# Batch-normalised matmul on one core: two output blocks turned by DMA, one more chunk of x copied apart, and a re-timed, re-ranked instruction plan

## The chip, the core and the metric

The kernel runs on one core of one Trainium2 chip. Its engines work side by side, each through its own list of instructions in order: TensorE (PE, matmuls and transpositions by matmul), VectorE (DVE), ScalarE (ACT), GpSimd (POOL) and SyncE (SP). Here SP's list holds nearly nothing but DMA issues (all stores and all transpositions by DMA); POOL's list holds the loads of x and of the weight beside its arithmetic. Sixteen DMA engines carry the transfers. The metric is the device time of one execution in microseconds, smaller being better; the median of three runs of the kernel before is 205.97 us (205.72 to 206.15).

## The reference

```
x: (16, 512, 1024) f32      weight: (1024, 768) f32      gamma, beta: (768,)
y      = matmul(x, weight)                       # 8192 rows x 768 columns
mean   = y.mean over all 8192 rows; var = y.var over all 8192 rows   (per column)
out    = gamma * (y - mean) / sqrt(var + eps) + beta
```

No output column can be written before all 8192 rows of that column are computed, since the mean and the variance run over all of them. x has 33.5 MB, the output 25.2 MB.

## The kernel before, in words

**Tiling.** The 8192 rows are cut into 16 chunks of 512 (C, CH), the 768 columns into 6 tiles of 128 (NT). All matmuls run in bf16. Columns 0 to 255 (tiles 0 and 1, "GA") are computed with rows on the partitions (`mm_rows`, L510, 256 columns wide); their sums are kept on DVE and POOL, and for the last two chunks they are computed with columns on the partitions (`ga_unit`, L814). Tiles 2 to 5 are computed with columns on the partitions: 8 matmuls of 512 rows for each chunk and tile (`mm`, L575), statistics by DVE (L711) or, for tile 2, partly by ACT (L720, L724), and a copy of y to SBUF in bf16.

**Loads and turning of x.** POOL's DMAs load x chunk by chunk and cast it to bf16 (`load_x`, L403). DVE turns it in 32x32 blocks so that k lies on the partitions (`turn_x`). For most chunks the turn moves pairs of bf16 as one 32-bit word, so in the result the two values of a pair lie next to each other and a matmul reads x with a step of two elements. Chunks in SINGLE (2, 3, 6) are turned value by value and read with step one. Chunks in PARTED (4, 5, 7 to 10) are copied apart after the turn: `part_chunk` has four ACT copies (L547) from `xT_sb` to `x_pl`, and all later matmuls of that chunk read `x_pl`. Chunks 12 to 15 (LATE) are copied apart later, by ACT or DVE. Chunks 0, 1 and 11 are read in pairs for all tiles.

**From y to the output.** Tiles 2 to 5 hold columns on the partitions and have to be turned back by 128x128 blocks. The unit is a block of two chunks (1024 rows, 512 KB of output). Three ways are used (`col_block`, `raw_turn`):
- "pe": normalise on DVE, 8 transpositions on TensorE into PSUM (`turn_block`, L1044; they may be threaded one by one between matmuls of other work, "hosted"), ACT copies PSUM to the f32 ring (L1210), SP stores.
- "xact": normalise (ACT for tile 2, DVE for tiles 3 and 4), one DMA transposition on SP's queue (L1220) from SBUF to SBUF, ACT converts bf16 to f32 (L1232), SP stores (L1202).
- RAW: the raw y is turned by a DMA transposition first (L1106), and normalised afterwards with rows on the partitions by DVE (L1174) and POOL (L1178), stored at L1182.

Before the change tile 2 has chunks 0-1 and 2-3 raw and its other blocks "xact", tile 3 has chunks 0-1 raw and the others "xact", and tile 4 has chunks 0-1, 2-3 and 4-5 raw and its other blocks "pe", the last one held back for the end ("held", L1252). Tile 5 is the tail: after the last matmul (L753) its statistics are closed, and all 16 chunks are normalised (L1348), turned on TensorE (L1044), copied by ACT (L1361) and stored (L1364). Columns 0 to 255 need no turning: DVE multiplies (L937), POOL or DVE adds (L942), SP stores (L946).

**What sets the order.** The kernel first collects some 790 tasks. Each has a priority, the engines it may run on with a time (busy, then until its result can be used), the tasks it waits for, and the buffers that it takes and uses. `arrange` plays these tasks through on a model of the five engines and of the DMA (`Wires`): again and again it takes the engine that can begin first, and of the tasks that can begin on it within 0.2 us the one with the smallest priority. The resulting list is the order in which instructions are written, engine by engine, and the chip keeps that order. So a changed duration or priority changes no work, only which instruction stands before which on each engine and each queue. Priorities are mostly due times: `clock`, which adds up TensorE's planned time, plus an offset. Turns of x have -1000 added, so that they always rank first.

**Buffers.** Turned chunks of x, parted copies and the tail's output share 12 buffers (XT); PSUM has 8 banks; the ring in SBUF holds loads of x and blocks of output.

Of the kernel before, what the change touches and what calls it, by code (L numbers as in the profile page):

```python
# [9 lines left out]
class Task:  # L10
# [3 lines left out]
    def __init__(self, prio, engines, emit, deps=(), dma=None, uses=(), takes=()):  # L14
# [6 lines left out]
        self.slack = self.look = 0.0  # L21
        for slot in self.uses + self.takes:
            slot.users.append(self)
# [74 lines left out]
class Wires:  # L98
# [4 lines left out]
    def __init__(self):  # L103
        self.free = 4.3
        self.lanes = {"SP": [], "POOL": [], "ACT": []}
# [5 lines left out]
    def send(self, queue, t, hold, took, count):  # L111

        soft = queue == "POOL"
        for _ in range(count):
            t = max(t, self.ready(queue)) + hold / count
            self.free = max(self.free, t + (1.0 if soft else 0.5)) + took / count
            land = self.free + (1.3 if soft else 0.6)
            self.lanes[queue].append(land)
        return t, land


def arrange(tasks, turns, log=None):
# [8 lines left out]
    SEM, LOOK = 0.06, 0.2  # L131
# [36 lines left out]
    while left:  # L168
# [46 lines left out]
        if t.dma:  # L215
            free[e], t.end = wires.send(e, start, occ, t.dma, t.count)
# [11 lines left out]
def kernel(  # L228
# [46 lines left out]
    PARTED, LATE, SINGLE = (4,5,7,8,9,10), (12,13,14,15), (2,3,6)  # L275
    MODE = {2:'xact',3:'xact',4:('pe',)*8}
# [98 lines left out]
    STORE, XBAR = 1 / 350.0, 1.25  # L375
# [72 lines left out]
    for kind, n, *n1 in order:  # L448
# [12 lines left out]
        if m0 == M // 2:  # L461
# [5 lines left out]
            t, {"POOL": (2.68 * rows / CH + 0.535 * also, 2.68 * rows / CH + 0.535 * also)}, load_x(m0, rows, slot, between),  # L467
# [5 lines left out]
        for i in range(rows // QR):  # L473
            c, q = divmod(m0 // QR + i, QPC)
            for j0, j1 in ((0, JW // 2), (JW // 2, JW)) if m0 < CH else ((0, JW),):
                new = q == 0 and j0 == 0
                x_ready[c, q, j1] = task(
                    -1000 + t, dve((2.2 if c in SINGLE else 1.16) * (j1 - j0) / JW + 0.02),
# [5 lines left out]
        if rows % QR:  # L484
# [4 lines left out]
                -1000 + t, dve(0.63), turn_x(slot, x_slot[c], m0, t0, 0, JW, False, P),  # L489
# [159 lines left out]
    def rows_stats(c, ts, slot, t):  # L649
# [30 lines left out]
        s = task((now + 4.2 if c < RC - 2 else 0), {"POOL": (1.36, 1.36 + 0.05), "DVE": (0.62, 0.7)}, add_squares, [a],  # L680
# [124 lines left out]
    def ga_unit(nt, c, q, cols=QR):  # L805
# [26 lines left out]
        b = task(clock[0] - late, dve(0.609 * cols / CH + 0.05), bn, [t], uses=[slot])  # L832
        mine = [h[1] for k, h in ga_half.items() if k[1] == c]
        k = task(clock[0] + 3.4, act(0.48 * cols / CH + 0.03), keep, [b] + mine,
# [20 lines left out]
    merges.append(task(U, dve(0.36), merge(0), [k[1] for k in ends], True))  # L855
    merges.append(task(U, pool(0.65), merge(1), [k[2] for k in ends]))
    for h in range(2):
        merges.append(task(U, pool(0.65), more(h), merges[1:]))
# [59 lines left out]
    s1 = task(U, pe(0.9), sums_rows, merges, takes=[tot_slot])  # L918
    se = task(U, dve(0.8), sums_entry, [s1], True, uses=[tot_slot])
    ag = [task(U, dve(0.25), aggregate_rows(a), [se] + [h[0] for k, h in ga_half.items() if k[0] == a]) for a in range(GA)]  # L920
    rt = task(U, {"ACT": (0.2, 0.3)}, root_rows, ag)
    sc = task(U, dve(0.3), scale_rows, [rt], True)
    sr = task(U + 0.1, dve(0.35), shift_rows, [sc], True)
    p0 = task(U, pe(0.45), spread_rows(0), [sc], takes=[a0_slot])
    p1 = task(U, pe(0.45), spread_rows(1), [sr], takes=[a1_slot])
    p1.look = 0.6
    sh = task(U, act(0.3), shift_sbuf, [p1], uses=[a1_slot])


    def rows_out(c, s0, s1, k):  # L930
# [19 lines left out]
        a = task(due, dve(0.3 * n), norm, [p0] + keeps, takes=[slot], uses=[y_row[c], a0_slot])  # L950
        b = task(due + 0.4, dve(0.3 * n) if k in ADDED else pool(0.59 * n), add, [a, p1 if k in ADDED else sh],
                 uses=[slot, a1_slot] if k in ADDED else [slot])
        task(due + 1.0, {"SP": (0.38, 0.4)}, store, [b], dma=n * NA * P * 4 / 1024 / 365.0 * 1.024,
# [14 lines left out]
    def finish_tasks(nt):  # L968
# [41 lines left out]
        if nt in ASTAT:  # L1010
            deps = [task(now + 1.0, {"ACT": (1.2, 1.3)}, total, deps)]
        a = task(now + 1.0, dve(0.5), var, deps)
        b = task(now + 1.0, {"ACT": (0.2, 0.3)}, root, [a])
        if nt > GA:
            return task(now + 1.0, dve(0.55), affine, [b], True)
# [396 lines left out]
```

## Time and profile before

| quantity | value |
|---|---|
| timed runs | 205.97 us median, 205.72 to 206.15 |
| span of the profiled execution (its first to its last instruction) | 204.1 us |
| the median less that span | 1.9 us |
| PE busy | 189.3 us (93%), 1210 matmuls and transpositions |
| DVE, ACT, POOL busy | 159.3, 146.2, 124.1 us |
| chain that ended last | PE 86%, ACT 3%, DMA 3%, POOL 2% |
| HBM read, written | 36.71 MB, 25.17 MB |
| mean granted TensorE clock | 0.979 |
| ACT copies apart, L547 | 32, mean 1063 ns (8 more on DVE, mean 715 ns) |
| ACT conversions after a DMA transposition, L1232 | 13, mean 1063 ns |
| ACT copies after TensorE's turning, L1210 | 4, mean 1014 ns |
| TensorE transpositions of tiles 4 and 5, L1044 | 104 |
| DMA transpositions L1220, issue to landing | 13, median 4.4 us |
| stores of 512 KB from the ring, issue to landing | 37, median 3.4 us |

How to read it: times are in microseconds from the start of the span. An engine's busy time counts its own instructions alone. The chain is followed back from the last instruction to what released it, each time, so what stands in it is what the end hangs on. The DMA share is the mean share of 16 engines, and because packets overlap it can pass 1; where transfers are of one kind the GB/s tell better whether the engines are full. Before 100 us the loads run, from 110 us on the stores.

### The profile page before, as it was taken

The numbers are of one execution on the slowest core, as the hardware profiler recorded it, in microseconds if no ns is written. First come the engines' busy times: TensorE is split into PE (matmuls) and PEld (weight loads), VectorE is DVE, ScalarE is ACT, GpSimd is POOL, SyncE is SP. The second block draws the span as 40 slices with busy tenths as digits, with TensorE's granted clock in tenths as the row PEclk, the third lists the DMA queues.
The fourth block names the chain that finished last, engine by engine and source line by source line (L and its number), as shares of the span: only waits on it lengthen the run. The fifth ranks groups of instructions, "written<-read, shape, count | busy, mean of one in ns | idle before, by whom it ended". The sixth has DMA issues, their size and how long they took to land.

```text
span 204.1 us, 3510 instructions
## 1 busy us (share of the span) xinstructions
PE 189.3 (93%) x1210; PEld 114.5 (56%) x1210; DVE 159.3 (78%) x250; ACT 146.2 (72%) x260; POOL 124.1 (61%) x150
## 2 busy tenths in 40 slices
PE   7969999999999999999999999999999999997900
PEld 3457554657488888777865444444444445544600
DVE  4031879999999999969989998987999878657900
ACT  2001461368989999899978766999998959956950
POOL 7776954877499989997403999389613312940000
PEclk9999999999999999999999999999999999999965
DMA  4999999999999999999686899899999999999998
GB/s 71 172 199 196 176 196 196 196 197 197 190 193 197 197 196 196 196 197 195 103 181 200 297 339 336 248 301 328 295 322 227 336 303 274 347 343 310 310 347 253
DMA packets 98562, 48.74 MB, mean 239 GB/s; under 512 B 24304, under 2 KB 98032, under 8 KB 98544
## 3 DMA queue, kind: packets, MB, share of 16 engines
q0 software_dynamic: 34624, 18.36, 65.5%
q1 hardware_dynamic: 63920, 30.16, 52.6%
q8 instruction: 9, 0.15, 0.3%
q14 instruction: 9, 0.07, 0.1%
HBM read 36.71 MB, written 25.17 MB: 303 GB/s over the span
## 4 chain that ended last, share of the span: by engine, by line
PE 86%; ACT 3%; DMA 3%; POOL 2%; issue 1%; ACTq 0%; DVE 0%; POOLq 0%
PE y_ps L575 54%; PE y_ps L510 24%; PE y_ps L814 4%; ACT o_sb L1361 3%; DMA ring<-in_x_dram 3%; PE o_ps L1044 1%; POOL ring L403 1%; POOL w_sb L387 1%; PE y_ps L753 1%; PE a_ps L903 1%; PE o_ps L1074 0%; ACTq L1407 0%; PE idle_ps L591 0%; PE tot_ps L871 0%; ACT ring L1252 0%
## 5 line engine op out<-in xcount | busy, mean ns | idle before, releaser
L575 PEld LDWEIGHTS <-w_sb 128*128 128x128 bf16 x520 | 50.3, 97 | 57.6
L575 PE MATMUL y_ps<-xT_sb,w_sb 128*128 128x512 bf16 (+1 forms) x272 | 59.3, 371 | 0.0
L575 PE MATMUL y_ps<-x_pl,w_sb 128*128 128x512 bf16 x248 | 57.4, 379 | 0.0
L403 POOL DMA_DIRECT2D ring<-in_x_dram x76 | 47.2, 626 | 14.4 <-DMA ring<-in_x_dram 5.5
L510 PE MATMUL y_ps<-w_sb,xT_sb 128*128 128x256 bf16 x448 | 50.6, 273 | 1.7 <-DMA ring<-in_x_dram 1.6
L510 PEld LDWEIGHTS <-xT_sb 128*128 128x128 bf16 x448 | 43.5, 98 | 9.4 <-DVE xT_sb L435 2.9
L435 DVE STREAM_TRANSPOSE xT_sb<-ring 128x1024 f32<-128x1024 f32 (+1 forms) x29 | 31.2, 1111 | 14.1 <-DMA ring<-in_x_dram 13.9
L711 DVE BATCH_NORM_STATS2 stats<-y_ps 128x6 f32<-128x512 f32 x46 | 30.9, 687 | 7.7 <-PE y_ps L575 7.2
L715 ACT CAST y_sb<-y_ps 128x512 bf16<-128x512 f32 x51 | 29.0, 593 | 10.4 <-DVE stats L711 6.3
L547 ACT COPY x_pl<-xT_sb 128x1024 bf16<-128x1024 bf16 x32 | 32.8, 1063 | 1.7 <-DVE xT_sb L435 1.7
L942 POOL TENSOR_TENSOR ring<-ring,sum 128x1024 f32<-128x1024 f32 (+1 forms) x11 | 23.8, 2188 | 14.9 <-ACT y_ps L724 10.9
L659 ACT ACTIVATE sq_sb<-y_ps 128x512 f32<-128x512 f32 x28 | 16.3, 610 | 16.2 <-PE y_ps L510 15.9
L666 POOL TENSOR_TENSOR sum<-sum,sq_sb 128x512 f32<-128x512 f32 x20 | 25.6, 1278 | 3.0 <-ACT sq_sb L659 1.7
L662 DVE TENSOR_TENSOR sum<-y_ps,sum 128x512 f32<-128x512 f32 x28 | 18.9, 675 | 6.3 <-ACT sq_sb L659 5.3
L672 ACT CAST y_sb<-y_ps 128x512 bf16<-128x512 f32 x28 | 16.3, 594 | 8.2 <-DVE sum L662 8.0
L1178 POOL TENSOR_TENSOR ring<-ring,sum 128x1024 f32<-128x1024 f32 x6 | 14.8, 2477 | 9.8 <-issue 8.5
L937 DVE TENSOR_TENSOR ring<-y_sb,a_ps 128x1024 f32<-128x1024 bf16 (+1 forms) x16 | 16.7, 1079 | 0.1
L1044 PE MATMUL o_ps<-ident,y_sb 128*128 128x128 bf16 x104 | 13.1, 221 | 1.6 <-DVE y_sb L1348 1.5
L1232 ACT CAST ring<-ring 128x1024 f32<-128x1024 bf16 x13 | 13.8, 1063 | 0.6 <-DMA ring<-y_sb 0.6
L1145 POOL COPY sum<-sum 32x256 f32<-32x256 f32 (+1 forms) x17 | 5.8, 340 | 13.4 <-DVE sum L1142 6.5
L428 DVE STREAM_TRANSPOSE xT_sb<-ring 128x2048 bf16<-128x2048 bf16 x6 | 13.5, 2290 | 0.1
L591 PE MATMUL idle_ps<-idle_sb 128*128 128x512 f32 x18 | 9.6, 688 | 1.5 <-DVE idle_sb L316 1.5
(104 smaller groups left out, 153.7 us busy)
## 6 DMA issues: line engine op xcount, KB each, us to landing
out_dram<-ring SPq DMA_DIRECT2D x37, 512.0 KB, 3.4
ring<-in_x_dram POOLq DMA_DIRECT2D x52, 256.0 KB, 8.8
out_dram<-o_sb SPq DMA_DIRECT2D x6, 512.0 KB, 4.7
ring<-in_x_dram POOLq DMA_DIRECT2D x16, 128.0 KB, 5.9
w_sb<-in_weight_dram POOLq DMA_DIRECT2D x8, 192.0 KB, 6.2
out_dram<-ring SPq DMA_DIRECT2D x6, 256.0 KB, 3.0
ring<-in_x_dram POOLq DMA_DIRECT2D x4, 192.0 KB, 7.8
out_dram<-o_sb SPq DMA_DIRECT2D x3, 256.0 KB, 2.5
```

Source lines behind the costliest of these rows:

```text
L403: bi = seq(nc.gpsimd.dma_start(x_bf[32 * i:32 * i + 32], src[:, :, KQ * i:KQ * (i + 1)]))
L435: seq(nc.vector.transpose(dst, src[:, :, jw0:jw1]))
L510: seq(nc.tensor.matmul(y_ps[:, s], x_of(c, jw, e, t * P, (t + 1) * P), w_sb[:, jw, e, 0:NA], start=(s == 0 and jw == 0 and e == 0), stop=( ...
L547: seq(nc.scalar.copy(dst, pairs) if eng == "ACT" else ENG[eng].tensor_copy(dst, pairs))
L575: seq(nc.tensor.matmul(y_ps, w_sb[:, jw, e, nt * P:(nt + 1) * P], moving(c, jw, e, q0 * QR, q1 * QR, parted), start=(jw == 0 and e == 0 an ...
L659: seq(nc.scalar.activation(sq_sb[:, 0:n], slot.tile[:, 0:n], AF.Square))
L662: seq(nc.vector.tensor_add(sum1, slot.tile[:, 0:n], sum1))
L666: seq(ENG[eng].tensor_add(acc, acc, state["sq"][:, 0:n]))
L711: seq(nc.vector.bn_stats(dst, slot.tile))
L715: seq(nc.scalar.copy(y(nt, c), slot.tile))
L937: seq(nc.vector.tensor_mul(slot.o, y_row[c].y[:, s0:s1], aff[0][:, None, :].to_broadcast([P, n, NA])))
L942: seq(ENG[eng].tensor_add(slot.o, slot.o, row[:, None, :].to_broadcast([P, n, NA])))
```

## The change

Four things are changed together.

1. MODE of column tile 4: blocks 3 and 4 (chunks 6-7 and 8-9) go from "pe" to "xact". Blocks 0 to 2 stay raw, 5 to 7 stay "pe" (7 held). So 16 transpositions leave TensorE and two transpositions by DMA join SP's queue, each with an ACT conversion in place of an ACT copy from PSUM.
2. PARTED gains chunk 11: four more ACT copies after chunk 11 is turned, and the matmuls of chunk 11 in tiles 2 to 5 read the copy.
3. The planner's durations and its DMA model get other numbers: the delay of a semaphore, the load's issue time, merges, statistics, normalisations, stores, and a model of its own for a DMA transposition.
4. After all tasks are made, 126 of them, by their number, get another priority (`NUDGE`). Counting the tasks in the order in which they are made, the numbers fall on loads and turns of x, row and column units on TensorE, statistics and copies on DVE and ACT, copies apart, the output blocks of columns 0 to 255, and the tail's normalisations and turns.

```diff
-    def send(self, queue, t, hold, took, count):
-
-        soft = queue == "POOL"
+    def send(self, queue, t, hold, took, count, turned=False):
+
+        if turned:
+            t = max(t, self.ready(queue))
+            self.free = max(self.free, t + 0.722) + took
+            land = max(self.free + 0.375, t + hold + 1.4)
+            self.lanes[queue].append(land)
+            return max(t + hold, land - 2.325), land
+        first, last = (1.095, 1.0425) if queue == "POOL" else (0.722, 0.441)
...
-    SEM, LOOK = 0.06, 0.2
+    SEM, LOOK = 0.03, 0.2
...
-    PARTED, LATE, SINGLE = (4,5,7,8,9,10), (12,13,14,15), (2,3,6)
-    MODE = {2:'xact',3:'xact',4:('pe',)*8}
+    PARTED, LATE, SINGLE = (4,5,7,8,9,10,11), (12,13,14,15), (2,3,6)
+    MODE = {2:'xact',3:'xact',4:('pe','pe','pe','xact','xact','pe','pe','pe')}
...
-    STORE, XBAR = 1 / 350.0, 1.25
+    STORE, XBAR, TURN = 1 / 345.85, 1.12, {"SP": (1.143, 1.143)}
...
-            part_chunk(c, clock[0] + (4.0 if c < EARLY else 20.0), act(1.05))
+            part_chunk(c, clock[0] + (4.0 if c < EARLY else 20.0), {"ACT": (0.946, 1.056)})
...
-        b = task(due + 0.5, {"SP": (1.4, 1.4)}, xbar, [a], dma=XBAR,
+        b = task(due + 0.5, TURN, xbar, [a], dma=XBAR,
                  takes=[t_slot] + ([slot] if MODE[nt][c // GY] == "xact" else []), uses=[yslot])
+        b.turned = True
...
+    NUDGE = {
+        12: 31, 14: 32.7, 16: 43, 17: 33, 20: 37, 23: 39, 28: 68, 29: 54, 31: 59, 38: 106, 45: 80, 50: 99,
+        51: 81, 56: 88, 57: 84, 58: 84, 90: 119, 97: 47, 110: 60, 125: 36, 129: 9, 133: 24, 134: -1, 137: -7,
...
+    }
+    for i, prio in NUDGE.items():
+        tasks[i].prio = prio
     order = arrange(tasks, turns)
```

More of the change, by code (lines that the diff above doesn't have):

```diff
@@ L215, in arrange @@
         if t.dma:
-            free[e], t.end = wires.send(e, start, occ, t.dma, t.count)
+            free[e], t.end = wires.send(e, start, occ, t.dma, t.count, t.turned)
         t.start, t.engine = start, e
@@ L466 @@
         load = task(
-            t, {"POOL": (2.68 * rows / CH + 0.535 * also, 2.68 * rows / CH + 0.535 * also)}, load_x(m0, rows, slot, between),
+            t, {"POOL": (2.57 * rows / CH + 0.6 * also,) * 2}, load_x(m0, rows, slot, between),
             dma=(rows * K * 4 / 1024 + 384 * also) * PER_KB * 1.024, takes=[slot])
@@ L1014, in finish_tasks @@
         if nt > GA:
[L1015 removed]
+            return task(now + 1.0, {"DVE": (0.78, 0.87)}, affine, [b], True)
         d = task(now + 1.0, dve(0.1), invert, [b])
@@ L1158, in keep @@
             seq(nc.scalar.copy(a_ps[:, 0:2 * P], row.rearrange("p i n -> p (i n)")))
-        d = task(now, dve(0.35), turn, [fin_task], True)
-        g = task(now, {"POOL": (0.8, 0.85), "ACT": (0.9, 1.0)}, gather, [d])
-        s = task(now, {"POOL": (1.2, 1.25), "ACT": (1.0, 1.1)}, deal, [g])
-        t = task(now, act(0.4), keep, [s], takes=[bank])
+        d = task(now, {"DVE": (0.467, 0.543)}, turn, [fin_task], True)
+        g = task(now, {"POOL": (0.98, 1.036), "ACT": (0.91, 1.02)}, gather, [d])
+        s = task(now, {"POOL": (1.43, 1.48), "ACT": (1.15, 1.25)}, deal, [g])
+        t = task(now, {"ACT": (0.302, 0.38)}, keep, [s], takes=[bank])
         raw_aff[nt] = bank, t, s, row[:, 1]
```

64 lines of the change are left out of this document (33 added, 31 removed), and 11 rows, old and new, of the table NUDGE.

## The prediction

> **What bounds the kernel now.** I read the chain of waits first, since it says which engine the end hangs on. Start, length and name:
>
> ```profile
> 5.98 6.13 DMA ring<-in_x_dram
> 12.14 1.03 PE y_ps L510 x8
> ...
> 14.99 0.86 PE idle_ps L591 x2
> ...
> 18.61 1.91 PE y_ps L510 x16
> ...
> 25.93 1.92 PE y_ps L510 x16
> 27.85 7.23 PE y_ps L575 x32
> ...
> 104.94 1.73 PE y_ps L575 x8
> ...
> 109.95 0.45 PE o_ps L1074 x8
> ...
> 184.80 1.81 PE y_ps L753 x16
> 186.62 0.24 PE o_ps L1044 x4
> ```
>
> TensorE starts at 12.14 us and is on the chain without a break until 186.86; no wait in between is longer than 0.07 us. So inside these 174.7 us a re-ordering alone can win almost nothing: only fewer or faster TensorE instructions shorten them. The same lines hold the prices. A matmul of 512 columns takes 7.23/32 = 0.226 us where x still lies in pairs (chunk 1) and 1.73/8 = 0.216 us where it was copied apart; a 128x128 transposition takes 0.45/8 = 0.056 us.
>
> Second, busy time, clock, DMA share and GB/s by stage, to see what else is full:
>
> ```profile
> 100.00:110.00 10.00, 10.00 (x80) 7.13 (x80) 8.79 (x28) 8.04 (x25) 0.00 (x0) 1.00 0.59 134
> 110.00:130.00 20.00, 20.00 (x97) 8.74 (x95) 18.89 (x23) 15.41 (x45) 16.72 (x8) 1.00 0.89 315
> 130.00:155.00 25.00, 25.00 (x117) 11.26 (x116) 22.69 (x40) 24.32 (x35) 16.64 (x19) 1.00 1.11 309
> 155.00:158.00 3.00, 3.00 (x16) 1.30 (x14) 3.00 (x6) 2.40 (x5) 0.00 (x0) 1.00 1.20 154
> 158.00:172.00 14.00, 14.00 (x75) 6.68 (x74) 11.13 (x25) 11.34 (x21) 3.90 (x4) 1.00 1.19 318
> 172.00:173.00 1.00, 1.00 (x10) 0.53 (x8) 1.00 (x2) 1.00 (x3) 0.00 (x0) 1.00 0.36 101
> 173.00:187.50 14.50, 14.06 (x92) 7.71 (x90) 9.51 (x17) 10.16 (x17) 7.07 (x3) 1.00 1.15 346
> 187.50:191.50 4.00, 2.87 (x33) 1.88 (x34) 3.76 (x14) 3.49 (x10) 0.00 (x0) 1.00 0.85 253
> 191.50:202.50 11.00, 2.59 (x33) 1.73 (x32) 2.14 (x7) 5.17 (x7) 0.00 (x0) 0.69 1.15 347
> 168.50:169.50 1.00, 1.00 (x7) 0.50 (x6) 0.97 (x6) 0.67 (x3) 0.00 (x0) 1.00 1.28 287
> 118.00:120.00 2.00, 2.00 (x10) 0.86 (x9) 2.00 (x3) 1.29 (x4) 2.00 (x2) 1.00 1.09 384
> ```
>
> Columns: window, length, PE, PE's weight loads, DVE, ACT, POOL, clock, DMA share, GB/s. The DMA engines are the second bound. Storing starts near 110 and moves 384 GB/s where full (118 to 120) with the wide rows of the first 256 columns, later 346 with rows of 512 bytes. From 158 to the last packet at 202.5 they are full but for short holes: in 172-173, 1 - 101/346 = 0.7 us; in 187.5-191.5, 4 x (1 - 253/347) = 1.1 us. Earlier: in 110-130, 20 x (1 - 315/384) = 3.6 us, and in 155-158 about 3 x (1 - 154/287) = 1.4 us, where a transposition hung. The last row but one is nearly pure transposition: 287 GB/s.
>
> Third, the SyncE queue, which issues all stores and transpositions:
>
> ```profile
> 168.72 1.71 SPq L1220 DMA_TRANSPOSE ring<-y_sb  x1
> 171.78 4.47 SPq L1202 DMA_DIRECT2D out_dram<-ring  x4
> ```
>
> It stands free from 170.43 to 171.78, just where the changed blocks' transpositions would go.
>
> **The change part by part.** The profiled span is 204.1 us; the median of the timed runs, 205.97, lies 1.9 above it, and I add that to every span.
>
> *Two blocks of column tile 4 (chunks 6-7 and 8-9).* Removed from TensorE: 2 x 8 transpositions x 0.056 = 0.90 us, all of it on the chain, as they are threaded between matmuls with nothing else running on PE. Added: 2 DMA transpositions. Each moves 128 x 1024 bf16 = 262 KB; at 287 GB/s that is 0.91 us, and with the start of each I take 1.0, so 2.0 us of all 16 DMA engines (ends: 0.76 each at the store rate, 346; 1.7 each, the SyncE time at L1220). The 512 KB stores stay. The Trainium skill (Advanced Engine Details and Errata, X-Bar Transpose (TRN2)) calls transposing DMAs as fast as regular ones; by it the pair would cost 2 x 262/346 = 1.5 us, but this trace shows 287 against 346 GB/s, and the measurement decides. On SyncE the pair adds 2 x 1.7 = 3.4 us of issuing in front of the four L1202 stores and the three of the raw blocks; the free 1.35 us covers part, and the rest costs nothing as long as several stores are already queued at the engines, which the 346 GB/s of 173-187.5 says. ACT copies from SBUF (L1232, mean 1063 ns) in place of PSUM (L1210, 1014 ns): +0.1 us for both. Each block now takes its ring space before the transposition, 4.4 us (median to landing) earlier than before; DVE already waits 1.8 us in 3 times at L1174 for stores to free ring space, so two more such waits are 0 to 1.2 us of DVE, which in 173-187.5 is busy 9.51 of 14.5: nothing.
>
> *Chunk 11 copied apart.* Four column tiles x 8 matmuls x (0.226 - 0.216) = 0.32 us off the chain. Added: four ACT copies at L547 (mean 1063 ns; three in a row end after 2.97, so 0.99 each in a row), 4.0 us of ACT, which must end before chunk 11's matmuls of column tile 2. ACT has 10 - 8.04 = 1.96 free in 100-110 and 4.6 in 110-130, so about 3.9 by 118. Cost taken: nothing (ends 0 and 2.0, below); in 130-155 the ACT is at 24.32 of 25, so copies that slip there have no cover.
>
> *Durations in the planner and the 126 priorities.* They add no work; they change the order on every engine and queue: several loads of x on POOL's queue are put later or earlier (the last 128 rows now rank before the 384 ahead of them), second-half turns of x on DVE lose their absolute rank, chunk-12 matmuls of tile 2 rank earlier, one SyncE transposition of tile 2 (chunks 6-7) ranks far later. What it can win on the chain is bounded: the filler at 14.99 (0.86) and two slow starts (1.91 and 1.92 against 16 x 0.109 = 1.75, together 0.3), 1.2 us in all; after the last matmul, 4.19 MB at 347 GB/s is 12.1 us and cannot shrink. What it can lose has no bound in the trace but the density that the old order reaches; rows nearest are the waits above. I take 0: with TensorE dense before, a new order that feeds it as well gives the same; I keep -1.2 and +2.0 as ends.
>
> Sum: -0.90 - 0.32 = -1.22 on TensorE. Whether it reaches the end depends on the DMA: it must do 2.0 us more in a time 1.2 us shorter, so it needs 3.2 us of holes. Those behind 158 give 0.7 + 1.1 = 1.8; 1.4 of the 5.0 before 158 must be filled too, which the re-ranked first-256-column blocks (several of their DVE norms rank earlier) can do. I take it that they do. Span 202.9, time 204.75.
>
> **The rivals.**
> 1. *The DMA engines take it back.* For it: 346 and 347 GB/s from 173 to 202.5, 1.09 share in 118-120. If only the 1.8 us behind 158 are filled, the last packet comes 2.0 - 1.8 = 0.2 later: 206.2, no difference. It goes to the slower side when less than 1.6 us of holes fill; with half (0.9) the end is 1.1 later: 207.1. A transposition that hangs as in 155-158 (1.4 us at 154 GB/s) would be enough. Against it: the hole at 172 lies exactly where the new pair falls. The Trainium skill (VectorE: DVE Perf Modes, Rules for kernel authors) speaks for this rival: turn 128x128 on TensorE where the result may go to PSUM, as it may here. The rows agree on the price of one block (0.45 us of PE against 1.0 of the DMA), not on which of the two has room.
> 2. *ACT becomes the bound at column tile 2.* If the copies of chunk 11 land in 100-110, 4.0 - 1.96 = 2.0 us are short; PSUM banks come free later and TensorE stands for up to that: 205.97 - 1.22 + 2.0 = 206.75, slower. It decides when less than 2.4 us of ACT is free before chunk 11's matmuls. For it: 0.52 us is all that ACT waits per unit of 1.8 there; against: chunk 11 needs only the one tile by then, and the order may put other chunks first.
> 3. *The new order also removes the head's idle work*: -1.2 more, 203.55. For it: loads and first matmuls are re-ranked; against: the filler stays in the program and the first data lands by DMA.
>
> **How the numbers follow.** Forecast 0.50 (204.75, its own range 204.3 to 205.4). Rival 1 at no difference 0.15, at the slower end 0.13; rival 2 0.12; rival 3 0.10. A measurement here tells about 0.2% (0.4 us). Faster 0.50 + 0.10 = 0.60, same 0.15, slower 0.25. The range runs from rival 3 (203.6) to nearly rival 1's slower end (207.0), leaving out half of rival 3 and a good half of that end, 0.12.
>
> **What would show it.** Transpositions L1044 on PE 88 and not 104, L1220 fifteen, x_pl matmuls 280 and not 248, copies at L547 44 in place of 40 (ACT and DVE together); the last L753 matmul ends near 185.4 in place of 186.6 if the PE steps are right. GB/s of 110-130 above 315 and the hole near 172 gone if the DMA finds room; last packets still near 202.5 with TensorE done early would be rival 1; a PE gap between 105 and 130 with ACT at 100% would be rival 2. The prediction falls if TensorE shows any wait over 0.3 us between 12 and 185 or if the DMA is full from 130 to the end.

## The result and the profile after

The changed kernel takes 211.85 us (median of 6, 211.37 to 213.03) against 206.06 for the kernel before on the same chip: a ratio of 1.0298 (95% interval 1.0272 to 1.0324), 5.8 us slower. The forecast was 204.75, faster, with a range up to 207.0. It was wrong.

The page of the profiled execution, span, busy times and chain by engine:

```profile
span 209.7 us, 3454 instructions
...
PE 190.0 (91%) x1177; PEld 113.7 (54%) x1194; DVE 160.7 (77%) x253; ACT 149.3 (71%) x270; POOL 119.0 (57%) x141
...
PE 29%; DVE 19%; ACT 17%; DMA 12%; POOL 9%; issue 8%; ACTq 1%; SPq 0%; DVEq 0%; POOLq 0%
```

The chain was 86% TensorE before and is 29% now. The end hangs on a string of DVE, ACT, POOL and DMA steps, each waiting for the one before.

What TensorE waited for (engine, line, released by: total in us, times, longest), and, in the second block, what POOL waited for before it could issue loads of x. L517 is the old L510, L410 the old L403, and the DVE lines L435 and L442 are the old L428 (turn value by value) and L435 (turn by pairs):

```profile
PE y_ps L517 <- DVE xT_sb L442: 2.1, 3, 1.2
...
PE y_ps L582 <- ACT x_pl L554: 0.5, 1, 0.5
```

```profile
POOL ring L410 <- DVE xT_sb L435: 11.0, 3, 6.0
```

TensorE, which had no wait over 0.07 us from 12.14 to 186.86, now waits for turns of x. The loads are held up by turns as well: 11.0 us where it was 5.1 (and 0.6 for turns by pairs).

The load stage by window, the kernel before first and then the one after (length, PE, weight loads, DVE, ACT, POOL, clock, DMA share, GB/s):

```profile
61.00:67.00 6.00, 6.00 (x58) 5.36 (x56) 5.69 (x8) 5.92 (x11) 5.83 (x8) 1.00 1.45 197
...
78.00:81.00 3.00, 3.00 (x30) 2.59 (x28) 2.80 (x3) 2.98 (x6) 2.99 (x6) 1.00 1.45 195
81.00:87.00 6.00, 6.00 (x50) 4.61 (x48) 5.75 (x8) 5.49 (x10) 5.92 (x7) 1.00 1.45 196
```

```profile
61.00:67.00 6.00, 6.00 (x58) 5.36 (x56) 5.19 (x7) 5.66 (x9) 5.91 (x8) 1.00 1.22 150
...
78.00:81.00 3.00, 3.00 (x28) 2.58 (x28) 1.60 (x3) 3.00 (x6) 3.00 (x6) 1.00 1.07 128
81.00:87.00 6.00, 5.95 (x50) 4.76 (x50) 3.83 (x6) 5.90 (x10) 4.86 (x8) 1.00 1.35 178
```

Before, the loads ran at 195 to 197 GB/s in these windows and were over at 99.7 us. Now they fall to 150, 128 and 178 and run until 102.9.

The two moments that the rest hangs on are the scale of columns 0 to 255 on DVE (nothing can be normalised before it) and the first store on SyncE, each from its engine's timeline (start, length, what). Before:

```profile
106.28 0.16 DVE L895 TENSOR_TENSOR scale<-std,gamma_sb 128x2 f32<-128x2 f32 x1
```

```profile
109.10 0.40 SPq L946 DMA_DIRECT2D out_dram<-ring  x1
```

After:

```profile
110.78 0.16 DVE L902 TENSOR_TENSOR scale<-std,gamma_sb 128x2 f32<-128x2 f32 x1
```

```profile
113.86 0.40 SPq L1092 DMA_DIRECT2D out_dram<-ring  x1
```

So 4.8 of the span's 5.7 us are lost before the first store. From there to the end it is 209.74 - 113.86 = 95.9 us, against 204.07 - 109.10 = 95.0 before: another 0.9. (Of the four executions of one kernel below, the one with the swapped loads, two were disturbed, the profiled one among them: its time is that of the other two, and of its profile only large differences are read.)

The store stage's end, after (to compare with the rows from 173 on in the prediction):

```profile
175.00:187.00 12.00, 11.95 (x68) 5.92 (x68) 9.42 (x17) 8.90 (x16) 4.38 (x5) 1.00 1.19 315
187.00:192.00 5.00, 3.56 (x31) 2.45 (x28) 4.67 (x13) 3.10 (x8) 3.91 (x2) 1.00 1.10 329
```

The DMA is nearly full through the closing of the statistics, where it had 1.1 us free before (253 GB/s). From the end of the last statistics of tile 5 (L767, the old L760) at 190.98 to the end it takes 18.8 us, where it was 17.0.

### The profile page after: what moved, and what is told of

Same layout as the page of the kernel before. It is cut to its first block, busy times and chain, and to the rows that moved or that the text cites. A ratio compares the mean times of both kernels' runs of the same rounds, so it can differ in the third digit from the quotient of the medians.

```text
span 209.7 us, 3454 instructions
## 1 busy us (share of the span) xinstructions
PE 190.0 (91%) x1177; PEld 113.7 (54%) x1194; DVE 160.7 (77%) x253; ACT 149.3 (71%) x270; POOL 119.0 (57%) x141
## 4 chain that ended last, share of the span: by engine, by line
PE 29%; DVE 19%; ACT 17%; DMA 12%; POOL 9%; issue 8%; ACTq 1%; SPq 0%; DVEq 0%; POOLq 0%
PE y_ps L582 14%; PE y_ps L517 10%; DMA ring<-in_x_dram 6%; POOL ring L949 6%; ACT x_pl L554 4%; DMA out_dram<-ring 3%; ACT o_sb L1370 3%; DMA ring<-y_sb 3%; ACT y_sb L722 2%; DVE sum L669 2%; DVE stats L718 2%; ACT ring L1241 2%; PE y_ps L821 2%; DVE xT_sb L435 2%; POOL ring L410 2%
## 5 line engine op out<-in xcount | busy, mean ns | idle before, releaser
L582 PE MATMUL y_ps<-x_pl,w_sb 128*128 128x512 bf16 x271 | 62.7, 379 | 1.2 <-ACT x_pl L554 0.5
L410 POOL DMA_DIRECT2D ring<-in_x_dram x76 | 47.1, 626 | 18.7 <-DVE xT_sb L435 11.0
L517 PE MATMUL y_ps<-w_sb,xT_sb 128*128 128x256 bf16 x448 | 51.7, 273 | 2.4 <-DVE xT_sb L442 2.1
L582 PE MATMUL y_ps<-xT_sb,w_sb 128*128 128x512 bf16 (+1 forms) x232 | 52.6, 369 | 0.5
L517 PEld LDWEIGHTS <-xT_sb 128*128 128x128 bf16 x448 | 43.1, 98 | 12.6 <-DVE xT_sb L442 4.7
L442 DVE STREAM_TRANSPOSE xT_sb<-ring 128x1024 f32<-128x1024 f32 (+1 forms) x29 | 31.5, 1113 | 16.2 <-DMA ring<-in_x_dram 16.1
L554 ACT COPY x_pl<-xT_sb 128x1024 bf16<-128x1024 bf16 x35 | 35.6, 1060 | 0.0
L722 ACT CAST y_sb<-y_ps 128x512 bf16<-128x512 f32 x51 | 28.3, 594 | 7.2 <-DVE stats L718 2.8
L673 POOL TENSOR_TENSOR sum<-sum,sq_sb 128x512 f32<-128x512 f32 x18 | 23.3, 1292 | 5.8 <-ACT sq_sb L666 5.3
L679 ACT CAST y_sb<-y_ps 128x512 bf16<-128x512 f32 x28 | 16.2, 604 | 2.1 <-DVE sum L669 2.0
L1241 ACT CAST ring<-ring 128x1024 f32<-128x1024 bf16 x15 | 15.4, 1046 | 2.5 <-DMA ring<-y_sb 1.7
L435 DVE STREAM_TRANSPOSE xT_sb<-ring 128x2048 bf16<-128x2048 bf16 x6 | 13.6, 2288 | 0.0
L598 PE MATMUL idle_ps<-idle_sb 128*128 128x512 f32 x18 | 11.1, 779 | 1.5 <-DVE idle_sb L323 1.5
L1153 POOL COPY sum<-sum 32x256 f32<-32x256 f32 (+1 forms) x10 | 3.4, 336 | 15.2 <-ACT sum L1153 14.4
L1182 DVE TENSOR_TENSOR ring<-r_sb,a_ps 128x1024 f32<-128x1024 bf16 x6 | 7.3, 1215 | 2.5 <-ACT y_sb L722 1.7
```

The source lines that it names most:

```text
L410: bi = seq(nc.gpsimd.dma_start(x_bf[32 * i:32 * i + 32], src[:, :, KQ * i:KQ * (i + 1)]))
L435: seq(nc.vector.transpose(dst[:, :, jw0:jw1], src[:, :, jw0:jw1]))
L442: seq(nc.vector.transpose(dst, src[:, :, jw0:jw1]))
L517: seq(nc.tensor.matmul(y_ps[:, s], x_of(c, jw, e, t * P, (t + 1) * P), w_sb[:, jw, e, 0:NA], start=(s == 0 and jw == 0 and e == 0), stop=( ...
L554: seq(nc.scalar.copy(dst, pairs) if eng == "ACT" else ENG[eng].tensor_copy(dst, pairs))
L582: seq(nc.tensor.matmul(y_ps, w_sb[:, jw, e, nt * P:(nt + 1) * P], moving(c, jw, e, q0 * QR, q1 * QR, parted), start=(jw == 0 and e == 0 an ...
```

## The experiments

The theories, as the expectations name them. A: the re-ranked early priorities delay turns of x, a late turn keeps its ring space, and the loads run dry. B: the two transpositions and the ACT copies cost the time, by a full DMA and a full ACT. C: chunk 11's copy holds one of the 12 buffers for turned x, which the turn of the last chunk then lacks. D: in the store stage the DMA's end and TensorE's end are in balance, so each transposition more lengthens the end by its own time and TensorE's gain is lost.

One table for all runs, so that the sections can be short. "First store" and "end" are read from each profile, the stretch is their difference, and the transpositions are those issued after the first store. The ratio is to the kernel before on the same chip. Single executions of the kernel before spread from 205.4 to 206.9 us, and each kernel has one profile, so tenths of a microsecond between two stretches can be chance.

| kernel | time, us | ratio (95%) | loads end | scale | first store | stretch | transpositions after |
|---|---|---|---|---|---|---|---|
| before | 206.06 | 1 | 99.7 | 106.3 | 109.10 | 94.97 | 14 |
| new durations alone | 207.49 | 1.0072 (1.0053-1.0091) | 99.8 | 107.8 | 110.64 | 94.96 | 14 |
| + chunk 11 | 208.07 | 1.0093 (1.0063-1.0123) | 100.6 | 110.1 | 112.91 | 93.56 | 14 |
| + two blocks by DMA | 210.44 | 1.0212 (1.0179-1.0244) | 99.8 | 109.7 | 112.53 | 96.43 | 16 |
| + 126 priorities: after | 211.85 | 1.0298 (1.0272-1.0324) | 102.9 | 110.8 | 113.86 | 95.88 | 16 |
| after, tile 4 on TensorE | 210.21 | 1.0212 (1.0181-1.0244) | 102.5 | 110.6 | 113.66 | 94.87 | 14 |
| before, two blocks by DMA | 208.26 | 1.0118 (1.0084-1.0153) | 99.5 | 106.0 | 108.86 | 97.41 | 16 |
| before, one block by DMA | 207.22 | 1.0068 (1.0045-1.0091) | 99.2 | 106.2 | 108.97 | 96.34 | 15 |
| before, two fewer by DMA | 206.65 | 1.0038 (1.0022-1.0054) | 100.0 | 106.6 | 109.36 | 95.97 | 12 |
| before, one priority | 209.85 | 1.0201 (1.0185-1.0216) | 101.8 | 108.2 | 112.83 | 94.92 | 14 |

### The changed kernel without the 126 priorities

```diff
-    NUDGE = {
...
-    }
-    for i, prio in NUDGE.items():
-        tasks[i].prio = prio
     order = arrange(tasks, turns)
```

> The changed kernel without the 126 priorities: new durations, the two transposed blocks and chunk 11's copies stay. Theory A (the priorities delay the turns of x that free the ring, so the loads run dry near 61 to 66 and 78 to 86 us, and scale is ready at 111 instead of 106.4 us): the loads run at 195 GB/s throughout, scale is ready by 107.5, and the time is 205.5 to 207.5 us. Theory B (the two transpositions and the ACT copies of chunk 11 are the cost, by a full DMA and a full ACT): it stays above 209.

Measured 210.44 us. The loads ended at 99.8 with no hole, as A said. But scale came at 109.7, hardly sooner than with the priorities, and the time missed A's 205.5 to 207.5 and hit B's "above 209". So the priorities are the smaller part of the loss (1.4 us of the medians), and something else delays scale. (TensorE's last statistics close at 187.57 here, 0.5 us later than before, and the end comes 4.9 us later, so it is not TensorE's end that sets it.)

### The new durations alone

The changed kernel with the other three changes taken out:

```diff
-    PARTED, LATE, SINGLE = (4,5,7,8,9,10,11), (12,13,14,15), (2,3,6)
-    MODE = {2:'xact',3:'xact',4:('pe','pe','pe','xact','xact','pe','pe','pe')}
+    PARTED, LATE, SINGLE = (4,5,7,8,9,10), (12,13,14,15), (2,3,6)
+    MODE = {2:'xact',3:'xact',4:('pe',)*8}
...
-    NUDGE = {
...
-    }
-    for i, prio in NUDGE.items():
-        tasks[i].prio = prio
```

> The kernel before with the new durations alone: no priorities, tile 4 turned on TensorE as before, chunk 11 read in pairs. Theory A: the old priorities keep their slack, 205 to 206.5 us, within 0.3% of before. Theory B: the same, as nothing that it blames is there. A third theory (durations as traced leave no slack, so any late landing moves the whole plan): 207.5 or more, with waits of TensorE in the load stage.

Measured 207.49 us, the edge of the third theory. Scale is 1.5 us later, and the stretch after the first store is unchanged (94.96). In the load stage TensorE now has a wait that the old order did not have:

```profile
PE y_ps L517 <- DVE xT_sb L442: 1.1, 2, 0.9
```

The longer of the two stands at 85.5 us. The changed durations alone cost 0.7%. That the plan made with them leaves less room in front of the turns is argued from this wait; no run changed one duration at a time.

### Seven turns ranked first again

```diff
     NUDGE = {
-        12: 31, 14: 32.7, 16: 43, 17: 33, 20: 37, 23: 39, 28: 68, 29: 54, 31: 59, 38: 106, 45: 80, 50: 99,
-        51: 81, 56: 88, 57: 84, 58: 84, 90: 119, 97: 47, 110: 60, 125: 36, 129: 9, 133: 24, 134: -1, 137: -7,
...
+        12: 31, 14: 32.7, 17: 33, 20: 37, 23: 39, 29: 54, 45: 80, 51: 81, 57: 84, 90: 119, 97: 47, 110: 60,
...
```

The entries 16, 28, 31, 38, 50, 56 and 58 of the changed kernel go; the others stay.

> The changed kernel with seven of the 126 priorities undone: the second-half turns of chunks 2, 6, 7, 9, 13 and the two last turns of chunk 15 rank first again, as before. Theory A in its narrow form (these turns alone starve the loads): load gaps gone, scale ready near 108, time 206 to 208.5 us. If other priorities do it as well: over 209. Theory B: over 209 too, but then without load gaps.

Measured 214.03 us (1.0379, 1.0355 to 1.0404), slower still, so theory A in its narrow form missed. The holes at 61 to 67 are gone, but the loads end at 102.0, scale comes at 111.2, TensorE stands 2.4 us in the store stage, and the stretch is 99.1. Taking out some of the priorities moved the whole order, and this run says nothing on the turns alone.

### Two blocks by DMA, and nothing else

On the kernel before:

```diff
-    MODE = {2:'xact',3:'xact',4:('pe',)*8}
+    MODE = {2:'xact',3:'xact',4:('pe','pe','pe','xact','xact','pe','pe','pe')}
```

> The kernel before with one edit: blocks 3 and 4 of tile 4 go to the DMA's transposition; durations, priorities and chunk 11 as before. TensorE does 16 transpositions less, 0.9 us. Theory A has nothing to say; my prediction's main case would give 205.1, its rival (the DMA is full from 158 us on) 206.2 to 207.1. Theory B: 207.5 or more.

Measured 208.26 us, B's side and above the rival of the prediction. TensorE got its gain: the statistics of tile 5 close at 185.95 in place of 187.09, 1.14 us earlier, 0.24 of it because the first store is earlier. But the stretch is 97.4, 2.4 longer, although the hole at 187.5 to 191.5 that the prediction counted on is filled:

```profile
173.00:187.50 14.50, 12.94 (x80) 6.86 (x77) 10.66 (x21) 10.62 (x18) 7.07 (x3) 1.00 1.15 334
187.50:191.50 4.00, 3.96 (x48) 2.67 (x48) 4.00 (x14) 3.65 (x7) 0.00 (x0) 1.00 1.15 346
```

The second row was 253 GB/s before and is 346 now, and TensorE and ACT are through earlier, yet the last packet goes at 204.6 in place of 202.8. What goes so late is seen in the run with one block, below.

### New durations and chunk 11 copied apart

The changed kernel without the two blocks and without the priorities:

```diff
-    MODE = {2:'xact',3:'xact',4:('pe','pe','pe','xact','xact','pe','pe','pe')}
+    MODE = {2:'xact',3:'xact',4:('pe',)*8}
...
-    NUDGE = {
...
-    }
-    for i, prio in NUDGE.items():
-        tasks[i].prio = prio
```

> The kernel before with the new durations and chunk 11 copied apart; tile 4 on TensorE as before, no priorities. Against the kernel with the new durations alone (207.5 us, scale ready at 108.0): theory C (the copy of chunk 11 holds one of the 12 buffers for turned x, so the turn of the last chunk waits for an ACT copy to give one back, as 0.24 us <-ACT x_pl at 103.11 without the priorities shows): scale ready near 109.9, the time 208.8 to 209.6 us. If ACT's 4 us are covered and the buffers suffice: 0.3 us faster, 207.2.

Measured 208.07 us: scale at 110.1 as theory C said, but the time 0.7 us below its range. Against the durations alone the first store is 2.3 us later and the stretch 1.4 shorter; TensorE's last statistics close only 0.2 us later (188.85 against 188.62), so more output stands ready when storing begins. That this is what shortens the stretch is argued. The turn of the last chunk on DVE, in this kernel:

```profile
103.49 2.43 DVE L442 STREAM_TRANSPOSE xT_sb<-ring 128x1024 f32<-128x1024 f32 x3 [0.24 <-ACT x_pl L554]
```

It is released by an ACT copy apart, which is what gives a buffer back. In the kernel with the durations alone the same turn began at 100.60, with no such wait.

### One block by DMA

On the kernel before:

```diff
-    MODE = {2:'xact',3:'xact',4:('pe',)*8}
+    MODE = {2:'xact',3:'xact',4:('pe','pe','pe','xact','pe','pe','pe','pe')}
```

> The kernel before with one block of tile 4 (chunks 6-7) by DMA instead of two. TensorE -0.45 us, DMA +1.0. Theory D (before the change TensorE's end and the DMA's end are in balance, so every DMA transposition more lengthens the end by its whole time and TensorE's gain is lost): about half of the two blocks' 2.2 us, 206.9 to 207.3. If one fits in the holes: 205.6.

Measured 207.22 us, in theory D's range. The stretch is 96.34: 1.4 us more for the first transposition, 1.1 for the second. But it grows in another way than D has it. The end of the DMA, the kernel before first and then this one (columns as above):

```profile
202.50:203.00 0.50, 0.00 (x0) 0.00 (x0) 0.00 (x0) 0.00 (x0) 0.00 (x0) 0.50 0.45 132
```

```profile
202.00:202.50 0.50, 0.00 (x0) 0.00 (x0) 0.00 (x0) 0.00 (x0) 0.00 (x0) 0.50 0.77 229
202.50:203.00 0.50, 0.00 (x0) 0.00 (x0) 0.00 (x0) 0.00 (x0) 0.00 (x0) 0.50 0.15 43
203.00:203.50 0.50, 0.00 (x0) 0.00 (x0) 0.00 (x0) 0.00 (x0) 0.00 (x0) 0.50 0.07 22
```

The 16 DMA engines together move 347 GB/s, so 22 is one of them alone. Most of them are through by 202.4 here, earlier than before: the holes took this transposition, and TensorE's gain arrived. One engine goes on until 203.6. The single packets in the traces say the same: each store ends in 16 packets of 4 bytes, taken here as one for each engine, and for the last store they come at these times (us):

| kernel | most engines | last engine |
|---|---|---|
| before | 202.6 | 202.8 |
| before, one block by DMA | 202.2 | 203.6 |
| before, two blocks by DMA | 203.2 | 204.6 |
| before, two fewer by DMA | 203.8 | 203.9 |
| before, one priority | 205.5 | 206.5 |
| after, tile 4 on TensorE | 207.1 | 207.3 |
| after | 207.0 | 208.1 |

In the kernel before, too, one engine lags by 1.4 us, at 181 to 187, and it is level again by 190.6, within the hole of 187.5 to 191.5. With one and with two blocks this hole is filled (346 GB/s), and an engine still lags at the end. So the hole was not free: a lagging engine caught up in it.

### Two fewer by DMA

On the kernel before:

```diff
-    MODE = {2:'xact',3:'xact',4:('pe',)*8}
+    MODE = {2:'xact',3:('xact','xact','xact','pe','pe','xact','xact','xact'),4:('pe',)*8}
```

> The other way: the kernel before with two DMA transpositions of tile 3 (chunks 6-7 and 8-9) given back to TensorE. TensorE +0.9 us, DMA -2.0. Theory D (balance): the last matmul ends 0.9 later, the tail after it stays 17.0 us, the time is 206.9 to 207.2. If the DMA alone set the end before: 204.1 to 205.2, faster.

Measured 206.65 us, 0.4% slower: the direction of theory D, a little less than its 206.9. The last statistics close 1.15 us later (188.24), the rest after them is 17.1 as before, and the DMA now has room there:

```profile
187.50:191.50 4.00, 2.44 (x31) 1.64 (x28) 3.38 (x13) 3.16 (x9) 0.00 (x0) 1.00 0.58 174
```

So one transposition more and two fewer are both slower. The kernel before sits at the bend: with two fewer TensorE's end moves the whole DMA's end, with one more the DMA's last engine sets it.

### The changed kernel with tile 4 back on TensorE

```diff
-    MODE = {2:'xact',3:'xact',4:('pe','pe','pe','xact','xact','pe','pe','pe')}
+    MODE = {2:'xact',3:'xact',4:('pe',)*8}
```

> The changed kernel with the two blocks of tile 4 back on TensorE; new durations, chunk 11's copies and all 126 priorities stay. Theory D: scale as late as in the changed kernel (110.9 us), then the stretch from scale to the end shrinks from 98.8 to about 97.7: 210.5 to 211 us. If the transpositions are no cost in this order: TensorE's 0.9 us come back on top, 212.5 or more.

Measured 210.21 us, near theory D's 210.5 to 211. The load stage is as in the changed kernel (scale at 110.6), the stretch falls from 95.88 to 94.87. In the changed kernel's order the two transpositions cost 1.0 us of stretch, in the old one 2.4. By the table of the last engine, the lag is all of this 1.0: 1.1 us against 0.2, while most engines end no later with the two transpositions than without.

### Early and late priorities apart

Only numbers up to 340 kept (tasks up to scale), then only those above:

```diff
     NUDGE = {
...
+        257: 101, 261: 52, 262: -979, 273: 69, 281: 24, 300: 114, 317: 53, 320: 88,
     }
     for i, prio in NUDGE.items():
```

```diff
     NUDGE = {
...
+        343: 108, 346: 227, 349: 96, 355: 111, 361: 106, 364: 111.5, 367: 135, 370: 149, 379: 109, 389: 160, 391: 67.5, 392: 55,
...
     }
     for i, prio in NUDGE.items():
```

> The changed kernel with only those of the 126 priorities kept that belong to tasks up to scale (loads, turns, row units, copies apart: numbers up to 340); the later ones are undone. Theory A (the early priorities starve the loads and TensorE): loads end near 102.8 and scale comes at 110.5 to 111 us as in the changed kernel; without the late priorities' help the stretch after it is 99 us as without any priorities, 211.5 to 213 us. If the early priorities are harmless: 210.4 us, as without any, with loads ending at 99.8.

> The other half: only the later priorities (numbers over 340) are kept, the early ones are undone. Theory A: loads end near 99.8 and scale comes near 109.9 as without any priorities; if the late ones win the 1 to 2 us behind scale by themselves, 208.5 to 209.5 us; if they were only right for the order before them, 211 or more.

With the early ones alone 213.06 us (1.0362, 1.0333 to 1.0392), near A's 211.5 to 213: the loads end at 103.2, scale comes at 112.0 (1 us later than expected), the first store at 114.78, and the stretch is 96.4, as without any priorities. With the late ones alone 215.34 us (1.0462, 1.0414 to 1.0510): the loads are undisturbed (end 99.7, first store 113.32), but the stretch is 99.5. So the early priorities bring the late loads, and the late ones help only together with the early ones.

### Thirteen buffers for turned x

```diff
-    XT, YB, SQ = C - EARLY, 28, 3
+    XT, YB, SQ = C - EARLY + 1, 24, 3
```

On the kernel with new durations and chunk 11 copied apart.

> New durations and chunk 11 copied apart, as in the run that had scale at 110.25 us, but with 13 buffers for turned x in place of 12 (paid with 4 of the 28 buffers for y, so its later part may be slower and only the load stage is compared). Theory C (the copy of chunk 11 takes the buffer that the last chunk's turn needs): scale comes back to 107.8 to 108.3 us. If ACT's time is what delays it: it stays near 110.

Scale came at 108.25 us, not 110.09: with the buffer the delay by chunk 11 is gone but for 0.4 us, and ACT does the same copies. The last chunk's turn on DVE begins at 101.01, not at 103.49, and waits for no copy. Theory C holds for the load stage. (The later part is slower, as expected of the four buffers for y that paid for it: 214.35 us, one execution, with the first store at 118.7.)

### Chunk 11 turned value by value

```diff
-    PARTED, LATE, SINGLE = (4,5,7,8,9,10), (12,13,14,15), (2,3,6)
+    PARTED, LATE, SINGLE = (4,5,7,8,9,10), (12,13,14,15), (2,3,6,11)
```

> The kernel before with chunk 11 turned value by value, so that its matmuls read it with step one without a copy apart: no ACT copies, no extra buffer, but two turns on DVE of 2.29 us in place of 1.11, 2.4 us more of DVE in the load stage. TensorE gets the 0.33 us that the change aimed at. If DVE has that room: 205.7. Theory D says no loss at the DMA (none is added): 205.5 to 206.1. If DVE is too full there (37.1 of 40 us busy from 60 to 100): scale up to 2.4 later, 206.5 to 208.

On the kernel before. Measured 207.65 us (1.0089, 1.0073 to 1.0106): the full-DVE case. The loads end at 102.0, and TensorE's gain of 0.33 us goes under in a loss of 1.8 us of the medians.

### One priority of the 126

```diff
+    for i, prio in {28: 68}.items():
+        tasks[i].prio = prio
     order = arrange(tasks, turns)
```

> The kernel before with one priority of the 126: the second-half turn of chunk 6 (2.29 us on DVE) gets 68 in place of -952.8, as in the changed kernel. Theory A: the load of chunk 9, which takes the ring space that this turn gives back, is issued near 60 us in place of 56.5, the rate of 61 to 67 us falls from 197 GB/s towards 150, the loads end 0.5 to 1.5 us later, and the time is 206.2 to 207.2 us. If that load has slack: rate and time as before.

On the kernel before. Measured 209.85 us, 2.0% slower by one priority out of some 790: the place and the rate as expected, the price more than double, and the way to it another. POOL's issues in the kernel before, and then in this one (start, length, what, count, and the wait ahead):

```profile
56.44 2.57 POOL L403 DMA_DIRECT2D ring<-in_x_dram  x4 [2.21 <-DVE xT_sb L428]
```

```profile
58.17 1.27 POOL L666 TENSOR_TENSOR sum<-sum,sq_sb 128x512 f32<-128x512 f32 x1 [4.28 <-ACT sq_sb L659]
...
59.53 2.58 POOL L403 DMA_DIRECT2D ring<-in_x_dram  x4
```

Its window from 61 to 67, columns as above:

```profile
61.00:67.00 6.00, 6.00 (x58) 5.38 (x56) 5.63 (x7) 3.24 (x5) 6.00 (x9) 1.00 1.21 151
```

The load of chunk 9 is issued 3.1 us later, the rate from 61 to 67 drops from 197 to 151 GB/s, the loads end 2.1 us later, scale comes 1.9 and the first store 3.7 us later. The load does not wait for the turn here: on DVE that turn runs from 59.73 to 62.02, after the load was issued. POOL came to the load late because the new order puts a sum ahead of it, and the sum waits 4.28 us for ACT. So the time of issue that theory A expected came by a wait that it did not name. The other 1.8 us are lost between scale and the first store, where the order differs too. From there the stretch is the old one to 0.05 us, in part by chance: most DMA engines end 0.8 us sooner after the first store than before, and one lags by 1.0. In the changed kernel it is as theory A has it: the same load is issued at 59.35, behind a wait of 4.45 us for the value-by-value turn, and the same window has 150 GB/s:

```profile
59.35 5.10 POOL L410 DMA_DIRECT2D ring<-in_x_dram  x8 [4.45 <-DVE xT_sb L435]
```

### The last two loads swapped

```diff
+    for i, prio in {57: 84}.items():
+        tasks[i].prio = prio
     order = arrange(tasks, turns)
```

> The kernel before with one other priority of the 126: the load of the last 128 rows gets 84 in place of 94.45, so the 384 rows come last. Theory A, second part (the last turns then take 2.4 us behind the last landing and not 0.6 to 1.2): loads to scale takes 8 us or more in place of 6.8, scale near 107.5 to 109, 206.5 to 208 us. If PE's other work covers it: within 0.3% of before.

On the kernel before: 214.28 and 216.63 us (1.0473, 1.0406 to 1.0539), far above the 206.5 to 208 expected. By the profile, loads to scale took 6.9 us, not the 8 expected, but the loads themselves ended at 109.5. The priority moved more than the two loads, and in another way than I thought.

### A transposition moved ahead of the first store

```diff
-    RAW, RAWADD, RAWDUE = {2:(0,2),3:(0,),4:(0,2,4)}, {2:'POOL',3:'POOL',4:'POOL'}, {2:14.0,3:8.0,4:8.0}
+    RAW, RAWADD, RAWDUE = {2:(0,2),3:(0,2),4:(0,2,4)}, {2:'POOL',3:'POOL',4:'POOL'}, {2:14.0,3:8.0,4:8.0}
```

On the kernel before, with one block and with both blocks of tile 4 by DMA.

> The kernel before with one block of tile 4 (chunks 6-7) by DMA, and chunks 2-3 of tile 3 turned raw, so that one transposition moves out of the store stage into the nearly free 100 to 108 us. Theory D: transpositions after scale as many as before, the tail behind the last matmul back to 17.0 us, TensorE 0.45 earlier: 205.5 to 206.0 us. If it is the number of transpositions at all: as with one block alone, 207.2. If the raw block's POOL addition of 2.43 us and DVE's 1.21 have no room: over 207.5.

> The same with both blocks of tile 4 by DMA: one more transposition after scale than before. Theory D: the tail as with one block alone, 18.8 us, the time 206.8 to 207.3, about 1.0 below the two blocks alone (208.3). If the number at all counts: 208.3.

Measured 209.28 us (1.0167, 1.0150 to 1.0184) and 210.06 (1.0212, 1.0196 to 1.0227). Both expectations of D missed: the first has 14 transpositions after the first store, as the kernel before, and yet a stretch of 98.0. A window shows part of the reason, this kernel first and then the kernel before:

```profile
170.00:175.00 5.00, 5.00 (x33) 2.58 (x32) 3.67 (x10) 4.37 (x10) 1.35 (x3) 1.00 0.66 163
```

```profile
170.00:175.00 5.00, 5.00 (x39) 2.87 (x38) 3.66 (x7) 4.94 (x9) 2.67 (x4) 1.00 1.01 288
```

The DMA has less to send here, 163 GB/s at a share of 0.66 against 288 at 1.01. The work after the first store is not the DMA's transfers alone but transfers and holes, and a block finished another way moves the holes. The other part is again a lagging engine: for the last store most engines are through at 204.2, the last one at 206.0. With both blocks there is no such lag (206.8 to 206.9), and the stretch is still 98.9. So the number of transpositions after the first store alone does not give the stretch, and theory D does not hold as a rule.

No version beat the kernel before.

## Why the prediction was wrong, step by step

**What bounds the kernel.** The prediction read a dense TensorE from 12 to 187 us as the bound and the DMA as second. The densities were right, the ranking was not. In the run without the priorities TensorE closes its last statistics 0.5 us later than before and the end comes 4.9 later; with one priority it is 1.8 and 3.7. In the three other kernels with 14 transpositions whose blocks are finished as before (new durations alone, one priority, the changed kernel with tile 4 on TensorE) the end follows the first store at 94.9 to 95.0 us, however late that store is and whatever TensorE did before it. A 1.5, 3.7 or 4.6 us later first store came through whole (with one priority in part by chance, as said there). Where the filling of the stretch itself was changed, it moved a little: 95.5 with chunk 11 turned value by value, 93.6 with it copied apart. The chain of waits named one bound where TensorE and the DMA ended together.

**Priorities and durations, taken as 0 with ends of -1.2 and +2.0.** Nothing in the sum stood for this step, and it measured +2.8 us of the medians (1.4 and 1.4), outside its ends; only the two blocks, below, missed by more (+2.4 for -0.9). The argument "a new order that feeds TensorE as well gives the same" looked only at TensorE, and took its density as given. By the first store the order lost 1.54 us with the new durations alone, and 1.33 more with the priorities (113.86 against 112.53). I had listed the late second-half turns and the re-ranked loads and put no price on them. In the changed kernel a turn that waits holds ring space, a load waits for it on POOL's queue (4.45 us), and the DMA behind it runs at 150 GB/s. The priority of one such turn alone measured 3.7 us of span, 1.9 of it by scale, though there the load stood behind a waiting sum and not behind the turn.

**Chunk 11 copied apart: -0.32 us, copies at no cost, ends 0 and +2.0.** I priced ACT's time and forgot the buffer. Rival 2 named the right stage and the wrong cause: the last chunk's turn waits for a buffer, scale comes 2.3 us later, and with a thirteenth buffer it does not. Of these 2.3 us, 1.4 are won back in the store stage, so 0.9 us of span stay, 0.6 us of the medians.

**Two blocks by DMA: -0.90 us on TensorE, +2.0 us on the DMA, of which holes take enough.** TensorE's size was right: alone, its last statistics close 1.14 us earlier, 0.24 of it from an earlier first store. The holes behind 158 did fill (187.5 to 191.5 went from 253 to 346 GB/s, 172 to 173 from 101 to 175), and with one block most DMA engines end 0.4 us earlier than before, as the sum wanted; with two they end 0.5 later. What failed is that the sum took the 16 engines as one and the holes as free. One engine lags 1.4 to 1.5 us behind the others at the end, 1.2 to 1.3 more than before, because the hole in which it caught up is filled. That is all of the one block's loss and more than half of the 2.2 us by which two blocks alone lengthen the median. Rival 1 named the right engine, but its mechanism, holes that do not fill, is not what the runs show, and its slower end (207.1) lies below what the two blocks alone measured (208.26). The Trainium skill's rule that rival 1 cited (VectorE: DVE Perf Modes, Rules for kernel authors: turn 128x128 on TensorE where the result may go to PSUM) agrees with the one-block and two-block runs, 0.7% and 1.2% slower, but the run with two fewer is 0.4% slower too, so here the rule holds for what is added, not for what is there. Against the rate of an ordinary transfer that the Trainium skill states for transpositions (Advanced Engine Details and Errata, X-Bar Transpose (TRN2)) speaks the prediction's row of 287 GB/s, against 346 for stores; the longer end of these runs is no measure of that rate, since the lag is in it.

**The sum by parts, as measured.** In spans: durations +1.5, chunk 11 +0.9, two blocks +2.5, priorities +0.8, together 5.7; in medians +1.4, +0.6, +2.4 and +1.4, together 5.8. By place: first store +4.8 (1.54 + 2.27 - 0.38 + 1.33), stretch after it +0.9 (two transpositions up, chunk 11 and the late priorities down). The parts were added in this order; in another order they need not have the same sizes.

**What was to show it.** The counts came out (L1051 88, L1228 15, 44 copies apart; of the 280 x_pl matmuls the trace records 271). The last matmul of tile 5 ends at 190.1, not near 185.4, and the DMA moves 261 GB/s from 110 to 130, not over 315. The condition "TensorE waits over 0.3 us between 12 and 185" was met: 1.16 us at 74.3 and 0.56 at 87.5, most of the rest in the load stage too, whose reserves the prediction had not looked at; the one of 0.54 at 166.4, behind an ACT copy apart, is in the store stage.

What stays open: what makes one DMA engine lag, which of the changed durations costs the 1.5 us, and how much of the priorities' loss comes from each of the re-ranked turns and loads beyond the one that was tried.

## What to carry to other kernels

Where a trace shows one engine dense to the end, look for a second resource that ends with it before paying the first engine's time with the second's: here one transposition more and two fewer were both slower. Price a re-ordering at the buffers it keeps: a task that waits longer holds its input, and the loads behind it are what run dry. Count a buffer that a new copy takes as carefully as its engine time. And do not take a hole in the DMA as free room before looking at whether all its engines end together.

## What the runs showed of the hardware that I had not expected

The loads ran at 195 to 197 GB/s in the kernel before, whose issues of loads pause for 4 us before that (52.4 to 56.4); after a pause of 7 us in the issues (52.5 to 59.4 in the changed kernel) the rate is not simply zero and then full again, but 150 for 6 us although eight transfers are issued in a row from 59.35 to 64.45. The same window has 151 in the kernel with one priority changed. Why it recovers so slowly no run here shows.

One of the 16 DMA engines can lag behind the others by more than a microsecond, and the end waits for it: 1.4 us with one block by DMA, 1.5 with two, 0.2 in the kernel before. In these three runs the lag begins next to a packet of 16 KB in the queue of instructions (at 179.66, 180.67 and 179.80 us, 0.93 to 0.95 us long): the store that ends at 179.5, or at 178.7 in the kernel before, still has its 16 end packets together, and of the stores that follow one packet comes 1.4 to 1.5 us late. That the packet causes the lag is argued from the times; no run moved it. The transposition that hung at 155 to 158 in the kernel before did so beside such a packet as well (155.58, 1.10 us), and 17 of its own packets took 1.0 to 1.5 us.
